# One core: the GpSimd drain in the last gate pair is taken out

## The chip, the core and the metric

The kernel runs on one core of one Trainium2 chip. The metric is device time in microseconds; lower is better. The times given are medians over several executions. The profile is one further execution, taken with the hardware profiler. The engines are named as in the profile: PE is TensorE (PEld its weight loads), DVE is VectorE, ACT is ScalarE, POOL is GpSimd, SP is SyncE, which only issues DMAs here.

## The reference

One layer of a streaming encoder trunk, over 2048 frames of a new stream (the prompt) and 32 further frames of a running one (the sample), with 1024 features, in float32:

```python
def layer(h, p, ...):
    proj = rmsnorm(h, g_mix) @ w_in
    hA, bA, cA, zA, vB, zB = jnp.split(proj, [...], axis=-1)
    yA, new_conv = short_conv_mixer(hA, bA, cA, zA, conv_hist, conv_w, conv_b)
    yB, new_pool = pooling_mixer(vB, zB, pool_hist, pos, pool_w, pool_scale)
    h = h + jnp.concatenate([yA, yB], axis=-1) @ w_out
    gate = jax.nn.sigmoid(rmsnorm(h, g_ple) @ w_ple_gate)
    h = h + (p @ w_ple) * gate
    return h, new_conv, new_pool
...
    return rmsnorm(h, g_final), ...
```

The part of interest is the end: the gate product with `w_ple_gate`, the sigmoid, the product of `p @ w_ple` (called the embedding, e) with the gate, the sum with h, and the final `rmsnorm` with `g_final`.

## The kernel before

Frames are cut into 16 tiles of 128 and a short one of 32. The kernel has three stages, one behind the other: the input projection with both mixers, the output projection with the residual, and the gate with the final norm. Every large product takes float32 operands that are split in two parts, high and low, and is made of three products of parts (`FINE`). Two tiles are always taken together as a pair, and the 2 x 2 blocks of a pair's matrix product are formed with seven block products in place of eight, by sums and differences of the blocks (function `seven`). Its three accumulators in PSUM are X, Y and Z. `carry` copies an accumulator out while it is still to be added to, `out` takes the finished block.

In the gate stage a loop runs over pairs 0, 2, ..., 12 with `gate_ops` and `done_g`; the last pair, tiles 14 and 15, has its own function `last_pair`. `done_g(i)` closes tile i: ScalarE squares h and sums it (`sumsq`, L94), GpSimd makes 1/sqrt of the mean in two small instructions (`rstd_of`, L73 and L77), VectorE scales the row (L1592), and a DMA stores it. For tile 13 `done_g` is called from within the last pair, as its step 3 (`before`).

`last_pair` works with these pieces, whose lines the profile names:

- L1670 (VectorE): adds an accumulator in PSUM to the carried copy; L1666 (ScalarE): the sigmoid of the result.
- L1633 and L1634 (VectorE): embedding times gate, and its sum with h (`gated`).
- L1638 (ScalarE) squares half a row of h and sums it, and GpSimd adds the sums (L1641, L1643) and takes the root (L1650).
- L1646: h times `g_bc`, on GpSimd for the first half of tile 14 (named hg, in `rest`), else on VectorE.
- L109 (TensorE): the embedding product of tile 15 (e_l), in `second`, with the weights wl that L123 loads again in four pieces; L1717: the seventh block product, in two halves of 256 columns (`end`).
- L1657 and L1659: the final scaling on VectorE and ScalarE, and L1658 and L1660 the stores, by SP and by ScalarE's queue.

The order of each engine's instructions is set when the program is built: a scheduler orders them by readiness, and `tc.keep_in_program_order` (here `fixed`) pins single ones to their place in the program. Each engine works through its own list in order, and waits for others through semaphores. `nc.gpsimd.drain()` at L1695 stands in the body of `last_pair`, ahead of the call of `seven`, and is pinned as well. It waits on no semaphore and posts none. In GpSimd's list it lies between the root of tile 12 (L77) and the first step of tile 13 (L73). GpSimd's own DMAs all come earlier in its list; the last is the store of tile 5. At the end of the program each engine has a closing sequence (put down to L1847), which on GpSimd begins with a drain and then has a handshake with the other engines, in which SP has waited for all stores.

Of the kernel before, what the change touches and what calls it, by code (L numbers as in the profile page):

```python
# [36 lines left out]
def trunk(ctx, tc, x_p, x_s, c_conv, c_pool, p_p, p_s, g_mix, w_in, conv_w, conv_b, pool_w,  # L37
          pool_scale, w_out, g_ple, w_gate, w_ple, g_fin, y_p, y_s, sc_p, sp_p, sc_s, sp_s):
    nc = tc.nc
# [1264 lines left out]
    with ExitStack() as s2:  # L1304
# [308 lines left out]
        def last_pair(i, A, before):  # L1613
# [15 lines left out]
            fixed = lambda ins: tc.keep_in_program_order(ins)  # L1629
# [62 lines left out]
            def rest():  # L1692
                of_first(cols_of(0), nc.gpsimd)

            fixed(nc.gpsimd.drain())  # L1695

            def second(cols):

                ps = bank(f"e_l{cols.start}")[:, :cols.stop - cols.start]
                embed_product(ps, pps, wp, cols)  # L1700
                return ps
# [109 lines left out]
        for i in range(0, NT - 3, 2):  # L1811
# [8 lines left out]
            if i + 2 < NT - 3:  # L1820
                done_g(i + 1, h[1])
        last_pair(NT - 3, S[NT - 3], lambda: done_g(NT - 4, h[1], True))

# [27 lines left out]
```

## Time and profile before

| | us |
|---|---|
| median of 3 runs | 913.25 (912.74 to 914.73) |
| profiled execution | 915.29 |
| span in the profile, first to last instruction | 913.5 |
| PE busy | 894.5 (98%) |
| DVE busy | 703.3 (77%) |
| ACT busy | 460.2 (50%) |
| POOL busy | 151.8 (17%) |
| DMA moved | 198.52 MB, of it 68.62 MB on GpSimd's queue (q0) |
| granted TensorE clock | 0.999 |

The profiled execution's own time is 1.8 us above its span, for what lies around the first and last instruction. In a row of the timeline stand the start in us from the span's start, the time in us, engine, line, operation, output<-inputs with their shapes, a count, and in brackets the idle time ahead of it with the instruction that ended it; "issue" stands there where the profile shows no releaser. A name with a q (POOLq, SPq) is an engine's instruction queue: what it only issues or waits with. Buffer numbers are left out of names, so c_g is the carried copy of several blocks.

### The profile page before, as it was taken

What the parts mean: (1) busy time and instruction counts of PE and PEld (TensorE: products, weight loads), DVE (VectorE), ACT (ScalarE), POOL (GpSimd) and SP (SyncE); (2) the same over time, 40 slices, a digit from 0 to 9 for tenths busy, and PEclk for the clock granted to TensorE, in tenths of its full rate; (3) what the DMA queues carried; (4) which work ended last, traced back from release to release, by engine and by line L of the source; (5) the groups of instructions that cost most, each with busy time, mean ns of one, the idle gap of its engine ahead of it and who ended that gap; (6) DMA issues with size and microseconds to landing.
All of it is one profiled execution on the core that took longest, in us unless ns stands there. A gap on an engine that the chain in (4) does not pass through costs nothing. (4 is left out here: it accounts for less than half of the span.)

```text
span 913.5 us, 12177 instructions
## 1 busy us (share of the span) xinstructions
PE 894.5 (98%) x4174; PEld 721.9 (79%) x4174; DVE 703.3 (77%) x1158; ACT 460.2 (50%) x834; POOL 151.8 (17%) x290
## 2 busy tenths in 40 slices
PE   8999999999999999999999999999999999999995
PEld 6788888888888778877788886888787778778884
DVE  6899799897993788746677679956557978897875
ACT  7744555554443354433343375643435865555553
POOL 2210122222131023100000021211112211110011
PEclk9999999999999999999999999999999999999999
DMA  8155286856699676767754595778678965565553
GB/s 277 52 187 173 81 265 201 243 170 210 194 346 428 154 221 188 231 208 253 241 150 147 184 357 164 269 218 283 214 241 285 315 226 184 178 227 191 187 207 144
DMA packets 113387, 198.52 MB, mean 217 GB/s; under 512 B 13174, under 2 KB 70062, under 8 KB 112429
## 3 DMA queue, kind: packets, MB, share of 16 engines
q1 hardware_dynamic: 91309, 124.72, 42.5%
q0 software_dynamic: 19568, 68.62, 22.3%
q10 hardware_dynamic: 2448, 4.39, 1.3%
q8 instruction: 33, 0.54, 0.2%
q14 instruction: 29, 0.24, 0.1%
HBM read 132.53 MB, written 65.15 MB: 216 GB/s over the span
## 5 line engine op out<-in xcount | busy, mean ns | idle before, releaser
L185 PE MATMUL z_o<-wo,y_S 128*128 128x512 f32 x192 | 47.4, 389 | 0.0
L185 PE MATMUL x_o<-wo_T,y_S 128*128 128x512 f32 x192 | 46.4, 391 | 0.7 <-DVE c_o L1319 0.7
L646 PE MATMUL x_zab<-B,w_zab_S 128*128 128x512 f32 x192 | 46.8, 392 | 0.2 <-DVE w_zab_S L84 0.2
L185 PE MATMUL z_g<-wg,g_S 128*128 128x512 f32 x192 | 46.8, 391 | 0.0
L646 PE MATMUL z_zab<-B,w_zab_S 128*128 128x512 f32 x192 | 46.8, 391 | 0.0
L185 PE MATMUL x_o<-wo,y 128*128 128x512 f32 x192 | 45.2, 389 | 0.0
L185 PEld LDWEIGHTS x_o<-wo_T,y_S 128*128 128x128 f32 x192 | 35.8, 188 | 9.0 <-DVE c_o L1319 1.6
L646 PEld LDWEIGHTS x_zab<-B,w_zab_S 128*128 128x128 f32 x192 | 35.8, 188 | 8.9 <-DVE w_zab_S L84 0.6
L185 PEld LDWEIGHTS x_o<-wo,y 128*128 128x128 f32 x192 | 36.0, 188 | 7.7
L646 PEld LDWEIGHTS z_zab<-B,w_zab_S 128*128 128x128 f32 x192 | 35.8, 188 | 7.8 <-DVE w_zab_S L84 0.3
L185 PEld LDWEIGHTS z_o<-wo,y_S 128*128 128x128 f32 x192 | 36.0, 188 | 7.5
L646 PE MATMUL x_ch<-B,w_ch_S 128*128 128x512 f32 x168 | 41.9, 392 | 0.0
L185 PEld LDWEIGHTS z_g<-wg,g_S 128*128 128x128 f32 x192 | 35.8, 188 | 7.5 <-ACT c_g L1573 0.2
L646 PE MATMUL x_zbv<-B,w_zbv_S 128*128 128x512 f32 x168 | 40.9, 392 | 0.6 <-ACT zs L986 0.6
L646 PE MATMUL z_zbv<-B,w_zbv_S 128*128 128x512 f32 x168 | 40.4, 390 | 0.0
L646 PE MATMUL z_ch<-B,w_ch_S 128*128 128x512 f32 x168 | 40.4, 389 | 0.0
L646 PEld LDWEIGHTS x_zbv<-B,w_zbv_S 128*128 128x128 f32 x168 | 31.3, 188 | 8.3 <-ACT zs L986 1.0
L646 PEld LDWEIGHTS x_ch<-B,w_ch_S 128*128 128x128 f32 x168 | 31.3, 188 | 7.3 <-ACT U L986 0.4
L646 PEld LDWEIGHTS z_ch<-B,w_ch_S 128*128 128x128 f32 x168 | 31.5, 188 | 6.6
L646 PEld LDWEIGHTS z_zbv<-B,w_zbv_S 128*128 128x128 f32 x168 | 31.5, 188 | 6.5
L81 ACT CAST y_S<-y_fS 128x512 fp32r<-128x512 f32 x28 | 16.9, 619 | 25.3 <-PE x_o L185 10.9
L1592 DVE SCALAR_TENSOR_TENSOR h<-h,rstd_f,g_bc 128x1024 f32<-128x1024 f32 (+1 forms) x15 | 19.2, 1280 | 12.2 <-POOL rstd_f L77 12.2
(552 smaller groups left out, 2281.0 us busy)
## 6 DMA issues: line engine op xcount, KB each, us to landing
wn<-in_w_in_dram SPq DMA_DIRECT2D x24, 512.0 KB, 5.3
y<-y_d SPq DMA_DIRECT2D x16, 512.0 KB, 6.9
p_dT<-T POOLq DMA_DIRECT2D x15, 512.0 KB, 5.1
e<-e_d SPq DMA_DIRECT2D x15, 512.0 KB, 4.3
x<-in_x_prompt_dram SPq DMA_DIRECT2D x14, 512.0 KB, 6.1
B<-p_d POOLq DMA_DIRECT2D x3, 2048.0 KB, 16.0
B<-p_dT POOLq DMA_DIRECT2D x3, 2048.0 KB, 21.9
h_d<-x SPq DMA_DIRECT2D x12, 512.0 KB, 7.5
```

The lines of the kernel that those rows point to most:

```text
L81: ins = nc.scalar.copy(hi, src)
L185: nc.tensor.matmul(ps[:n], lhs[:, k, a, :n], w[b][:, k], start=start and k + q == 0, stop=k == KH - 1 and q == 2, skip_group_check=True)
L646: nc.tensor.matmul(ps, lhs[:, k, x], b[:, k, y], start=start and k + q == 0, stop=stop and k == KH - 1 and q == 2, skip_group_check=True)
L1592: nc.vector.scalar_tensor_tensor(h[:n], h[:n], rf[:n], g_bc[:n], op0=ALU.mult, op1=ALU.mult)
```

## The change

One line of `last_pair` goes, the drain on GpSimd:

```diff
             def rest():
                 of_first(cols_of(0), nc.gpsimd)
 
-            fixed(nc.gpsimd.drain())
-
             def second(cols):
```

Nothing else is edited. GpSimd's list around the place, before (ms_f and rstd_f are the two steps of the root, of tile 12 in the first two rows and of tile 13 in the next two; the list leaves out instructions that only wait, and so the drain, which stood behind the second row):

```order
L73 TENSOR_SCALAR ms_f_7892<-ssq_f_7890 128x1
L77 TENSOR_TENSOR rstd_f_7894<-ms_f_7892,nhalf 128x1
L73 TENSOR_SCALAR ms_f_7966<-ssq_f_7964 128x1
L77 TENSOR_TENSOR rstd_f_7968<-ms_f_7966,nhalf 128x1
L1641 TENSOR_SCALAR ssq_l_0_7986<-ssq_l_0_7986 128x1
L1646 TENSOR_TENSOR hg_7906<-h_7902,g_bc 128x512
```

And now:

```order
L73 TENSOR_SCALAR ms_f_7892<-ssq_f_7890 128x1
L77 TENSOR_TENSOR rstd_f_7894<-ms_f_7892,nhalf 128x1
L73 TENSOR_SCALAR ms_f_7965<-ssq_f_7963 128x1
L77 TENSOR_TENSOR rstd_f_7967<-ms_f_7965,nhalf 128x1
L1641 TENSOR_SCALAR ssq_l_0_7985<-ssq_l_0_7985 128x1
L1646 TENSOR_TENSOR hg_7906<-h_7902,g_bc 128x512
```

The rows are the same; only the running numbers of buffers behind the drain are lower by one, and line numbers behind it by two. The lists of the other four engines, DMAs among them, keep every instruction at its place as well. GpSimd's program has 431 instructions before and 430 now, five drains before and four now: one at the start (L1838) and three in the closing sequence (L1847).

## The prediction

> **What bounds the kernel now.** I read the page's busy shares first, then the windows by stage, then TensorE's waits in the last 50 us, and then the timeline of the last pair engine by engine.
>
> ```profile
> PE 894.5 (98%) x4174; PEld 721.9 (79%) x4174; DVE 703.3 (77%) x1158; ACT 460.2 (50%) x834; POOL 151.8 (17%) x290
> 780.00:889.00 109.00, 109.00 (x499) 87.68 (x499) 92.01 (x135) 59.27 (x104) 14.66 (x27) 1.00 0.57 196
> 889.00:913.50 24.50, 15.12 (x82) 12.61 (x80) 14.11 (x21) 9.25 (x21) 5.15 (x12) 0.95 0.42 153
> PE x_g L1717 <- DVE c_g L1670: 2.4, 1, 2.4
> ```
>
> TensorE bounds the kernel until the last pair: in 780 to 889 us it is busy for all of 109.00 us. Of the last 24.5 us it fills only 15.12. There the order of work decides, and TensorE has one wait that counts: 2.4 us before L1717, for VectorE's L1670. So the question is what made that L1670 late. The timeline has the chain (start, duration, engine):
>
> ```profile
> 891.29 0.69 DVE L1670 TENSOR_TENSOR c_g<-y_g,c_g 128x512 f32<-128x512 f32 x1
> 891.39 0.20 ACT L94 ACTIVATION_READ_ACCUMULATOR junk<-h 128x1 f32 x1
> 889.50 0.55 POOL L77 TENSOR_TENSOR rstd_f<-ms_f,nhalf 128x1 f32<-128x1 f32 x1
> 894.59 0.19 POOL L73 TENSOR_SCALAR ms_f<-ssq_f 128x1 f32<-128x1 f32 x1 [4.54 <-issue]
> 894.86 0.55 POOL L77 TENSOR_TENSOR rstd_f<-ms_f,nhalf 128x1 f32<-128x1 f32 x1
> 895.44 1.28 DVE L1592 SCALAR_TENSOR_TENSOR h<-h,rstd_f,g_bc 128x1024 f32<-128x1024 f32 x1 [3.47 <-POOL rstd_f L77]
> 896.65 0.68 DVE L1633 TENSOR_TENSOR c_g<-e,c_g 128x512 f32<-128x512 f32 x1
> 897.37 0.69 DVE L1634 TENSOR_TENSOR h<-h,c_g 128x512 f32<-128x512 f32 x1
> 897.97 0.69 DVE L1670 TENSOR_TENSOR c_g<-z_g,c_g 128x512 f32<-128x512 f32 x1
> 898.86 0.71 ACT L1666 ACTIVATE c_g<-c_g,rs_h 128x512 f32<-128x512 f32 x1
> 899.60 1.56 DVE L1633 TENSOR_TENSOR c_g<-e,c_g 128x512 f32<-128x512 f32 x1 [0.94 <-ACT c_g L1666]
> 901.08 0.68 DVE L1670 TENSOR_TENSOR c_g<-x_g,c_g 128x512 f32<-128x512 f32 x1
> 901.82 1.69 PE L1717 MATMUL x_g<-wq,g 128*128 128x256 f32 x12 [2.37 <-DVE c_g L1670]
> ```
>
> Read it backwards. L1717 follows the L1670 of X (901.08), which stands in VectorE's order behind all rows above it, down to the L1592 of tile 13 at 895.44. That one sat idle 3.47 us for GpSimd's rstd, and GpSimd's first step for it (L73) began at 894.59. Its input, ScalarE's sum of squares, was done at 891.39 + 0.20 = 891.59. So L73 came 3.0 us after its data, and its bracket names no releaser ("issue"). What stands between the two on GpSimd is the instruction that the change removes:
>
> ```profile
> 889.46 0.60 POOLq L1695
> L1695 POOLq DRAIN  x1: 5012/5012/5012, 889.5 to 889.5; - x1
> L1847 POOLq DRAIN  x3: 34/98/677, 908.4 to 913.3; - x3
> L1838 POOLq DRAIN  x1: 168/168/168, 0.3 to 0.3; - x1
> ```
>
> The first row is from the chain of waits, the others from the views by source line. The drain of L1695 ran from 889.46 to 894.47. Only 0.6 us of that is the pow at 889.50, which ended at 890.05; 4.42 us are left over. The other four drains of GpSimd took 0.03 to 0.68 us, and the 0.68 covers a running pow of 0.57.
>
> **The change part by part.** One instruction goes. Nothing else moves on any queue, and the DMAs keep their places, so there are two terms: what the drain held up, and where its 4.42 us go.
>
> *Term 1, the front.* Without the drain L73 follows its data as its twin for tile 12 does: about 0.09 us after the sum, 891.68. From L73 to VectorE's L1592 the rows above take 895.44 - 894.59 = 0.85 us, so L1592 starts at 892.53, when VectorE has been free since 891.29 + 0.69 = 891.98. Step by step from there: L1633 at 892.53 + 1.21 = 893.74 (its sigmoid, the first row below, ended at 892.74) and L1634 from 894.46 to 895.15. Then VectorE is ahead of TensorE and waits for Z:
>
> ```profile
> 892.01 0.73 ACT L1666 ACTIVATE c_g<-c_g,rs_h 128x512 f32<-128x512 f32 x1 [0.42 <-DVE c_g L1670]
> 893.32 2.95 PE L185 MATMUL z_g<-wg,g_S 128*128 128x512 f32 x12
> 896.11 1.98 PE L185 MATMUL x_g<-wg_T,g_S 128*128 128x512 f32 x8
> 897.92 1.52 PE L109 MATMUL e_l<-wl,pps_l 128*128 128x512 f32 x6
> 899.35 1.26 POOL L1646 TENSOR_TENSOR hg<-h,g_bc 128x512 f32<-128x512 f32 x1
> ```
>
> Z is ready at 893.32 + 2.95 = 896.27, so L1670 of Z starts at 896.33, the sigmoid at 897.05, L1633 at 897.80 and the L1670 of X at 898.43 (X was ready at 896.11 + 1.98 = 898.09), done at 899.12. L1717 could go at 899.18. TensorE itself is then the later one: the six products of e_l began at 897.92 and go at 0.227 us each (the eight before them took 897.92 - 896.11 = 1.81), so they leave TensorE at 899.28. L1717 moves from 901.82 to 899.28: **-2.54 us**. From there to the end each wait hangs on TensorE's products, then on ScalarE, GpSimd and the last stores, and all of it shifts along. Bounds: the idle that the row prints, 2.37, and 2.64 if L1717 could follow L1670 at once.
>
> One price in it needs a look. GpSimd's L1646 (hg) took 1.26 us at 899.35, and the VectorE L1633 that met it, with two inputs in SBUF, took 1.56 us in place of 0.68: it ended 0.55 us after hg did, so it had waited. In the changed run hg moves along with L1634, behind which it began 1.98 us later, to 896.44, and ends at 897.70, just before L1633 at 897.80. It meets the L1670 of Z, whose one input is in PSUM. For that pair I have these rows, a pow at its normal length while VectorE reads PSUM:
>
> ```profile
> 593.26 0.69 DVE L1319 TENSOR_TENSOR c_o<-x_o,x 128x512 f32<-128x512 f32 x1 [1.37 <-PE x_o L185]
> 593.68 0.55 POOL L77 TENSOR_TENSOR rs_h<-ms_h,nhalf 128x1 f32<-128x1 f32 x1
> ```
>
> So I take no delay. If hg did hold the L1670 of Z to its end, that would start 1.37 later (897.70 for 896.33), the chain would give L1717 at 900.4 or so and term 1 would shrink to about -1.42. The Trainium skill, "GPSIMD Engine Reference", section "1. Specifications", has GpSimd share its SBUF interfaces with VectorE and clash with VectorE instructions that have two SBUF inputs; by that rule the L1670 of Z goes free, as in the rows, and the sum stays as it is.
>
> *Term 2, where the 4.42 us go.* GpSimd still has a drain at the end, at L1847. Whether it inherits them depends on what the long drain waited for. Its last DMA lay far back (first row; the other two are the first and the last of the list of its DMA issues, which come to 148):
>
> ```profile
> 812.32 0.57 POOL L1593 DMA_DIRECT2D out_dram<-h  x1 [1.09 <-DVE h L1592]
> p_dT<-T POOLq DMA_DIRECT2D x15, 512.0 KB, 5.1
> ...
> out_dram<-g_bc POOLq DMA_DIRECT2D x1, 4.0 KB, 8.6
> ```
>
> What sets the long drain apart from the other four is this: ahead of it GpSimd had issued all its 148 DMAs of the run, and no earlier drain lay between. The drain of L1838 stands before the first DMA; those of L1847 have none since L1695. 4.42 us over 148 is 30 ns each, the size of a short software step. So I take it that a GpSimd drain goes through the DMAs issued since the last drain, at 30 ns each, and that the first drain of L1847 now pays it. At the end of the kernel stands:
>
> ```profile
> 908.44 0.57 POOL L1650 TENSOR_TENSOR rstd_l<-ssq_l,nhalf 128x1 f32<-128x1 f32 x1
> L1847 SPq DRAIN  x3: 7/7/7, 912.7 to 913.0; - x3
> L1847 POOLq EVENT_SEMAPHORE  x4: 17/17/17, 912.8 to 913.4; - x4
> ```
>
> The last pow ends at 909.01. The stores behind it are waited for by SP, whose drain at 912.7 lets GpSimd's closing handshake begin at 912.8; 0.7 us later the span ends. Shifted by 2.54 the stores would allow the handshake at 910.26. The inherited drain ends at 909.01 - 2.54 + 4.42 = 910.89, the handshake is at 910.93: 3.75 of the 4.42 us lie under the last stores, and **+0.7 us** stick out. Bounds: 0 if the drain is short there (0.68 with the pow, as before), and +1.3 if the whole recorded 5.01 counts from the end of the pow.
>
> Sum: -2.54 + 0.7 = **-1.84 us**. The profiled execution, 915.29 us around its span of 913.5, becomes 913.45. The median of the runs, 913.25, lies 2.04 below the profiled one; the same difference makes it **911.4 us**, 0.2% less.
>
> The Trainium skill, "VectorE: DVE Perf Modes", section "The DRAIN you can't avoid", speaks against a gain: it gives the preamble's and postamble's drains as about 12 ns, constant, on all five engines. On GpSimd the rows differ (34 to 677 ns there, 5012 at L1695); for SP, at 7 ns, they agree. By the rule the time would not change.
>
> **The rivals.**
>
> *The cost does not reappear.* The 4.42 us belong to the place, where weight pieces and a store were in flight (rows below), and not to a backlog. For: nothing proves the 30 ns. Against: that traffic was SP's, not GpSimd's own. Then only term 1 counts: 913.25 - 2.54 = 910.7.
>
> *Half of the gain is lost on the way.* Either hg holds VectorE, as worked out, or the store of tile 13, which now issues near 893.9, delays the last weight piece:
>
> ```profile
> 892.17 0.32 SPq L123 DMA_DIRECT2D wl<-wl_d  x1
> 896.76 0.34 SPq L1593 DMA_DIRECT2D out_dram<-h  x1
> wl<-wl_d SPq DMA_DIRECT2D x4, 512.0 KB, 5.5
> out_dram<-h SPq DMA_DIRECT2D x2, 512.0 KB, 2.6
> ```
>
> At the median of 5.5 the piece lands at 897.7, and the fifth product of e_l needs it at 897.92 + 4 x 0.227 = 898.83, so 1.1 us of delay are free; a store that pushed it back by its whole 2.6 would cost 1.5. With -1.42 or -1.04 in front and the +0.7 behind, the time is 912.5 to 912.9.
>
> *Nothing changes.* The drain is long only under the profiler, or L73 was held by something else and stays there: 913.25.
>
> *Slower.* A drain waits for every store in flight, SP's and ScalarE's too, and only then spends its 4.42 us. For: at L1695 the store of tile 12, issued at 891.40, would land at 894.0 by the median of 2.6, near the drain's end at 894.47, and weight pieces were in flight before. Against: it would leave 0.5 us after that landing, not 4.42. Then in the changed run the last drain starts its work when the last store has landed (912.7 - 2.54 = 910.2), ends at 914.6, and with 0.7 behind it the span is 915.4: +1.9, 915.1. It decides from the point where the drain ends more than 2.54 us after the stores. Its milder form, no gain in front and a drain of 4.42 from 909.01 to 913.43, gives +0.7, 913.95.
>
> **How the numbers follow.** Forecast 0.50 (its own range 910.9 to 912.0), cost does not reappear 0.23, half lost 0.07, nothing 0.04, slower 0.16. About 0.2%, 1.83 us, is what a measurement of this kernel can tell from no change. The forecast lies on that line; I give it 0.30 beyond and 0.20 within, because of term 2's bounds the smaller price (a drain of 0.68 at this very place) has been measured and the larger has not. Faster: 0.30 + 0.23 = 0.53. Within: 0.20 + 0.07 + 0.04 + 0.02 of the slower case's mild form = 0.33. Slower: 0.14. The range goes from 910.4 (cost does not reappear, less a third of a microsecond of spread) to 913.6, and leaves out most of the slower case.
>
> **What would show it.** In the changed profile L73 of tile 13 should start near 891.7 with a bracket that names ScalarE's L94, L1592 near 892.5, and L1717 near 899.3 with no wait for L1670 worth speaking of. Term 2 is right if GpSimd's first L1847 drain takes about 5 us and the closing handshake waits for it, wrong if that row stays at 0.68. The forecast is wrong from the start if L73 stays near 894.6.

## The result, and the profile after

| | before | changed |
|---|---|---|
| median, us | 913.25 (911.37 to 914.73, 6 runs) | 909.67 (909.16 to 911.01, 6 runs) |
| ratio of the times | | 0.9964, 95% interval 0.9951 to 0.9976 |
| profiled execution, us | 915.29 | 909.97 |
| its span, us | 913.5 | 908.2 |

The change is faster by 0.4%. The direction and the mechanism came as forecast; the time lies 1.7 us below the 911.4 and 0.7 us below the low end of the range.

First the last pair of the changed kernel, as a timeline (start, duration, engine, line, operation, and in brackets the idle time ahead with its releaser). Lines behind the change are lower by two, so L1717 of before is L1715 here:

```profile
886.10 0.55 POOL L77 TENSOR_TENSOR rstd_f<-ms_f,nhalf 128x1 f32<-128x1 f32 x1
886.27 2.88 PE L185 MATMUL z_g<-wg,g_S 128*128 128x512 f32 x12
887.97 0.19 ACT L94 ACTIVATION_READ_ACCUMULATOR junk<-h 128x1 f32 x1
888.24 0.19 POOL L73 TENSOR_SCALAR ms_f<-ssq_f 128x1 f32<-128x1 f32 x1 [1.59 <-ACT junk L94]
889.10 1.28 DVE L1592 SCALAR_TENSOR_TENSOR h<-h,rstd_f,g_bc 128x1024 f32<-128x1024 f32 x1 [0.53 <-POOL rstd_f L77]
...
892.90 0.69 DVE L1670 TENSOR_TENSOR c_g<-z_g,c_g 128x512 f32<-128x512 f32 x1 [1.19 <-PE z_g L185]
893.01 1.30 POOL L1646 TENSOR_TENSOR hg<-h,g_bc 128x512 f32<-128x512 f32 x1
894.39 0.69 DVE L1633 TENSOR_TENSOR c_g<-e,c_g 128x512 f32<-128x512 f32 x1 [0.79 <-ACT c_g L1666]
894.52 1.52 PE L109 MATMUL e_l<-wl,pps_l 128*128 128x512 f32 x6
894.99 0.69 DVE L1670 TENSOR_TENSOR c_g<-x_g,c_g 128x512 f32<-128x512 f32 x1
895.88 1.60 PE L1715 MATMUL x_g<-wq,g 128*128 128x256 f32 x12
902.41 0.57 POOL L1650 TENSOR_TENSOR rstd_l<-ssq_l,nhalf 128x1 f32<-128x1 f32 x1
```

The bracket of L73 now names ScalarE's sum of squares, where it said "issue" before: the instruction waits for its data and for nothing else. The bracket ahead of TensorE's seventh block product, 2.37 us before, is gone.

The two executions cannot be compared by clock times, since the changed one reached the last pair earlier. So I count from the first Z product of the last pair, at 889.70 before and 886.27 after. That product lies ahead of everything the drain holds up. The windows from there to the end of the span (busy time of PE, PEld, DVE, ACT, POOL, then the granted clock, DMA share and GB/s), first of before, then of the changed kernel:

```profile
889.70:913.50 23.80, 14.42 (x79) 12.04 (x77) 13.74 (x20) 9.25 (x21) 4.53 (x11) 0.95 0.40 149
```

```profile
886.27:908.20 21.93, 14.20 (x79) 12.10 (x77) 12.95 (x20) 9.36 (x21) 4.60 (x11) 0.91 0.44 161
```

The same work takes 23.8 us before and 21.9 after: **1.9 us less in the last pair**. The other 3.4 us of the difference between the two profiled executions lie ahead of it, where both kernels run the same program.

The closing sequence of the changed kernel, from its view by source line (count, then shortest, median and longest in ns, first and last start):

```profile
L1845 POOLq EVENT_SEMAPHORE  x4: 17/17/17, 907.5 to 908.1; - x4
L1845 POOLq DRAIN  x3: 46/98/5026, 902.4 to 907.9; - x3
L1845 SPq DRAIN  x3: 7/7/7, 906.7 to 907.7; - x3
```

The 5 us have moved here. SP was through with the stores at 906.7, but GpSimd's drain ran from 902.4 to 907.4, and the handshake began at 907.5. Before, SP was done at 912.7 and the handshake came at 912.8. So 0.7 us of the drain stick out.

### The profile page after: what moved, and what is told of

The parts are those of the page before. It is cut to its first block, busy times and chain, and to the rows that moved or that the text cites. A ratio compares the mean times of both kernels' runs of the same rounds, so it can differ in the third digit from the quotient of the medians.

```text
span 908.2 us, 12176 instructions
## 1 busy us (share of the span) xinstructions
PE 893.2 (98%) x4174; PEld 722.8 (80%) x4174; DVE 702.4 (77%) x1158; ACT 460.1 (51%) x834; POOL 152.0 (17%) x290
## 4 chain that ended last, share of the span: by engine, by line
PE 73%; issue 11%; DMA 8%; DVE 3%; ACT 2%; POOL 2%; POOLq 0%; DVEq 0%; ACTq 0%
PE x_g L185 9%; PE x_o L185 8%; PE x_zab L646 6%; PE x_zbv L646 6%; PE x_ch L646 6%; PE z_g L185 5%; PE z_o L185 4%; DMA raw_zab_0b<-in_w_in_dram 4%; PE z_zab L646 3%; PE z_ch L646 3%; PE z_zbv L646 3%; PE e L109 2%; PE y_g L185 2%; PE y_o L185 2%; DMA B<-p_d 2%
## 5 line engine op out<-in xcount | busy, mean ns | idle before, releaser
L81 ACT CAST y_S<-y_fS 128x512 fp32r<-128x512 f32 x28 | 17.0, 620 | 28.1 <-PE x_o L185 12.2
L1319 DVE TENSOR_TENSOR c_o<-x_o,x 128x512 f32<-128x512 f32 x14 | 9.6, 689 | 21.8 <-PE x_o L185 21.8
```

Of the source, the lines that this page charges most:

```text
L81: ins = nc.scalar.copy(hi, src)
L1319: add = lambda o, a, b: nc.vector.tensor_tensor(o, a, b, op=ALU.add)
```

## The experiments

In what follows "length" is the time from the first Z product of the last pair to the end of the span, and "L73" the start of tile 13's L73 counted from that product. "Left after the pow" is a drain's recorded time less 0.59 us: the drain is recorded from 0.04 us ahead of a pow of 0.55 us, and ended behind it in every run.

**The same program again, and the change again.** Two kernels, timed 12 times each beside 35 runs of before: before without any edit, and the change as it stands.

> The kernel before, unchanged, timed against itself: how far do two sets of runs of one program differ? Theory 1 (the drain accounts for 1.9 us of the 3.6, the rest is scatter between executions in the work ahead of the last pair): sets may differ by 1 to 2 us, a ratio up to 0.2% from 1. Theory 2 (taking the instruction out also makes the work ahead of the last pair faster by about 1.7 us, every time): sets of one program agree within 0.1%, 0.999 to 1.001.

> The changed kernel once more. Theory 1: the ratio comes nearer to 0.998 (-1.9 us) than 0.9964; the profile again shows -2.5 us up to the last product and a drain of about 5.0 us in the closing sequence. Theory 2: 0.996 again (-3.5 us), and in the profile a last pair that is 1.9 us shorter with the rest gained ahead of it.

Before, run again: median 913.65 us (912.0 to 917.93), ratio 1.0005 (0.9991 to 1.002). Its timeline, where the columns are as above:

```profile
886.72 2.88 PE L185 MATMUL z_g<-wg,g_S 128*128 128x512 f32 x12
891.63 0.19 POOL L73 TENSOR_SCALAR ms_f<-ssq_f 128x1 f32<-128x1 f32 x1 [4.54 <-issue]
898.86 1.70 PE L1717 MATMUL x_g<-wq,g 128*128 128x256 f32 x12 [2.38 <-DVE c_g L1670]
```

The first Z product stands at 886.72 with the drain still in the program, 3.0 us earlier than in the first profile of before and only 0.45 later than in the changed kernel. So those 3 us ahead of the last pair are scatter between executions: before reaches the earlier time too. Over half of it arises where the output projection gives way to the gate stage: between 700 and 740 us TensorE is busy for 38.4 us in the first profile of before, and for all 40 in this one and in the first of the change. Inside the last pair the two profiles of before agree: L73 at +4.91 (4.89 in the first profile), and with a span of 910.6 us the length is 23.9 (23.8). The two timed sets of before agree within 0.1%, which was theory 2's forecast for them; the change, run again, shows sets of one kernel further apart.

The change, run again: median 911.28 us (908.68 to 913.94), ratio 0.9971 (0.9959 to 0.9984). Its timeline:

```profile
886.32 2.88 PE L185 MATMUL z_g<-wg,g_S 128*128 128x512 f32 x12
895.93 1.60 PE L1715 MATMUL x_g<-wq,g 128*128 128x256 f32 x12
```

With a span of 908.2 us the length is 21.9, and the product follows at +9.61, as in the first profile of the change; the first drain of the closing sequence takes 5.03 us again. The six runs of the result had a mean of 909.80, these twelve 911.26: sets of one kernel differ by 1.5 us. The ratio of 0.9971 lies midway between the 0.998 of theory 1 and the 0.9964 of theory 2, so the timed sets decide for neither. The profiles speak for theory 1: the change is worth 1.9 us in the last pair, and before, run again, comes as early to that pair with the drain as the changed kernel without it.

**The place kept, the waiting taken out.** A one-element memset on GpSimd stands where the drain stood, pinned in the same way.

```diff
-            fixed(nc.gpsimd.drain())
+            fixed(nc.gpsimd.memset(warm, 0.0))
```

> In place of the drain a memset of one column on GpSimd (0.1 us): GpSimd's list is as long as before, but nothing is drained there. Theory 1: the time of the changed kernel within 0.1%; GpSimd's root for tile 13 follows its data by 0.1 to 0.3 us; closing drain 5.0 us. Theory 2 in the form that the length of GpSimd's list matters: 1.7 us slower than the changed kernel, about 911.4.

Median 910.73 us (908.79 to 914.46), ratio 0.9971 (0.9958 to 0.9983). The timeline:

```profile
886.98 2.88 PE L185 MATMUL z_g<-wg,g_S 128*128 128x512 f32 x12
887.27 0.10 POOL L1695 MEMSET warm<- 128x1 f32 x1
888.95 0.19 POOL L73 TENSOR_SCALAR ms_f<-ssq_f 128x1 f32<-128x1 f32 x1 [1.58 <-ACT junk L94]
```

An instruction at this place costs 0.10 us and holds nothing up; L73 comes at +1.97, as in the change, the closing drain takes 5.03 us, and with a span of 908.9 us the length is 21.9 again. It is the drain that held GpSimd, not the place or the pinning.

**The drain moved to where GpSimd is idle.** The old drain goes, and a new one stands behind the last DMA that GpSimd issues, after tiles 4 and 5, some 77 us ahead of the last pair.

```diff
-            fixed(nc.gpsimd.drain())
...
+            if i == 4:
+                tc.keep_in_program_order(nc.gpsimd.drain())
```

> The drain stands right behind GpSimd's last DMA (the store of tile 5, issued near 810 us), where GpSimd has nothing to do for about 12 us. Theory 1 (a GpSimd drain goes through the DMAs issued since the last drain, 148 here, about 30 ns each, and only once): the drain there takes 5 to 8 us unseen, the closing drain 0.7 us, the gain in front stays, and the time is 0.7 us below the changed kernel's. Rival (the cost belongs to the place, or the closing drain costs 5 us anyway): closing drain 5 us and the time of the changed kernel.

Median 910.61 us (909.42 to 913.13), ratio 0.997 (0.9958 to 0.9981). The first row is the moved drain, the second the closing sequence:

```profile
L1822 POOLq DRAIN  x1: 10131/10131/10131, 809.1 to 809.1; - x1
```

```profile
L1848 POOLq DRAIN  x3: 34/98/675, 902.5 to 907.3; - x3
```

The closing drain is back at 0.68 us, so one earlier drain takes the whole price off the end. Behind it GpSimd had nothing to do until 821, so the 10.13 us cost nothing. They are longer than the 5 us of the old place, and than the 5 to 8 that were expected. A store of GpSimd's was issued at 809.10, right ahead, and landed 7.9 us later, at 817.0; the drain ended at 819.2, 2.2 us behind it. Two kernels further down (0 DMAs between, and 16 tiny stores) have a drain at the same place:

```profile
L1823 POOLq DRAIN  x1: 7041/7041/7041, 810.1 to 810.1; - x1
```

```profile
L1823 POOLq DRAIN  x1: 6665/6665/6665, 809.5 to 809.5; - x1
```

There the same store was issued at 810.16 and 809.52 and took 4.8 and 4.4 us to land, and the drain ended 2.2 us after that in both. So a drain of GpSimd also waits for GpSimd's own stores that are still under way. From the first Z product at 886.38 the length of the kernel with the moved drain is 21.2, another 0.7 us less than in the change. That is the size of the piece that sticks out there. The timed runs don't separate the two kernels (910.61 and 911.28, intervals that overlap).

**What the drain counts.** My term 2 had 30 ns for each of 148 DMAs. The next kernels keep the drain at its old place and put a second one further ahead, so that a known number of GpSimd's DMAs lies between the two. The second drain stands behind the store of tile 5 (0 DMAs between), behind the store of tile 0 (8), ahead of the gate stage (22), and at the start of the output projection (50). Each kernel has one of these; the last line serves for the third and the fourth, at its two places:

```diff
+            if i == 4:
+                tc.keep_in_program_order(nc.gpsimd.drain())
...
+            if i == 0:
+                tc.keep_in_program_order(nc.gpsimd.drain())
...
+        tc.keep_in_program_order(nc.gpsimd.drain())
```

> Two drains: one right behind GpSimd's last DMA and the one of before at its place. Between them lie no DMAs. Theory 1 (30 ns for each DMA since the last drain, once): the drain at the old place ends within 0.1 us of the pow ahead of it, so it is about 0.6 us long; closing drain 0.7; from the start of the last pair's Z product to the end of the span 21.2 us, as with the early drain alone. Rival (the cost belongs to the place): 5.0 us again at the old place and 23.8 us.

> An extra drain behind the store of tile 0, with 8 DMAs of GpSimd between it and the drain at the old place. Theory 1: the drain at the old place ends 0.24 us + about 0.05 after the pow ahead of it; last pair 21.2 us. Rival (place): 4.4 us after it, 23.8 us.

> An extra drain at the start of the gate stage, with 22 DMAs of GpSimd between it and the drain at the old place. Theory 1: the drain at the old place ends 0.66 us + about 0.05 after the pow; last pair 21.2 us. Rival (place): 4.4 us after it, 23.8 us.

> An extra drain at the start of the output projection, with 50 DMAs of GpSimd between it and the drain at the old place. Theory 1: the drain at the old place ends 1.5 us + about 0.05 after the pow; that is at the time when the input of tile 13's root is ready, so the last pair is still 21.2 to 21.3 us. Rival (place): 4.4 us after it, 23.8 us.

The drain at the old place, in the views by source line of the four kernels in this order:

```profile
L1695 POOLq DRAIN  x1: 660/660/660, 887.5 to 887.5; - x1
```

```profile
L1695 POOLq DRAIN  x1: 1322/1322/1322, 885.7 to 885.7; - x1
```

```profile
L1697 POOLq DRAIN  x1: 2466/2466/2466, 887.6 to 887.6; - x1
```

```profile
L1696 POOLq DRAIN  x1: 4754/4754/4754, 888.2 to 888.2; - x1
```

Left after the pow are 0.07, 0.73, 1.88 and 4.17 us: 0.07 and then **82 ns for each DMA**, in a straight line, and not 30. The time hangs on GpSimd's DMAs since the last drain, so the backlog was right and its price was not. At 82 ns each, the 4.42 us of before are the price of 53 DMAs, not of 148. The lengths are 21.2, 21.2, 21.3 and 24.9 us, and the closing drain took 0.67 to 0.68 us in all four. The first three came within 0.1 us of the forecast. The 24.9, forecast at 21.2 to 21.3, did not: at 82 ns the drain held L73 until +4.64, and a part of the excess is of another kind (see the longer gap, below). One execution of each took 910.77, 908.96, 910.89 and 915.29 us, beside 913.85 of before.

**Count or bytes, and how many stay on the books.** Three kernels. In the first, sixteen stores of 4 bytes each are added behind the early drain, with the old drain kept. In the second, the same sixteen are added to before without an early drain (164 DMAs in all). In the third, a second drain is put into the input projection, so that 64 DMAs follow it and 84 precede it. The edits of the first and the third (the second has the first without its drain):

```diff
+            if i == 4:
+                tc.keep_in_program_order(nc.gpsimd.drain())
+                scr = tc.dram_tile([16, 8], F32, name="scr")
+                for k in range(16):
+                    tc.keep_in_program_order(nc.gpsimd.dma_start(scr[k:k + 1, :1], nhalf[:1, :1]))
...
+                if gi == 1 and j == 3:
+                    tc.keep_in_program_order(nc.gpsimd.drain())
```

> Drain early and at the old place, as in the run with both, and between them 16 extra DMAs of GpSimd of 4 bytes each (they write to a scratch tensor that nothing reads). The runs so far gave 0.07 us after the pow for 0 DMAs, 0.73 for 8, 1.88 for 22, 4.17 for 50: 0.082 us each. By the count of DMAs: 0.07 + 16 x 0.082 = 1.38 us. By their bytes or pieces (one piece each, where the 8 had 128 rows of 4 KB): under 0.2 us.

> The kernel before with the same 16 DMAs of 4 bytes ahead of the drain, and no early drain. With all 148 DMAs the drain took 4.42 us after the pow, which is 53 at 0.082. If a limit on the number of DMAs that are still on the books sets that, 4.42 again. If the limit is one of room that small DMAs hardly take up, up to 4.42 + 16 x 0.082 = 5.7 us. If every DMA counts and the first ones are only cheaper, 4.9 us (164 at 0.030).

> An extra drain late in the input projection, with 64 DMAs between it and the drain at the old place. Straight line: 0.07 + 64 x 0.082 = 5.3 us after the pow. Limit at about 53 DMAs: 4.42 us, as with 148.

The drain at the old place in the three, and in the last fence the added drain of the third:

```profile
L1695 POOLq DRAIN  x1: 1976/1976/1976, 889.6 to 889.6; - x1
```

```profile
L1695 POOLq DRAIN  x1: 6317/6317/6317, 886.7 to 886.7; - x1
```

```profile
L1697 POOLq DRAIN  x1: 5899/5899/5899, 885.6 to 885.6; - x1
```

```profile
L1294 POOLq DRAIN  x1: 4368/4368/4368, 380.8 to 380.8; - x1
```

| kernel | DMAs since the last drain | left after the pow, us | 0.07 + 0.082 x DMAs |
|---|---|---|---|
| drain behind tile 5 | 0 | 0.07 | 0.07 |
| drain behind tile 0 | 8 | 0.73 | 0.73 |
| 16 tiny stores | 16 | 1.39 | 1.38 |
| drain ahead of the gate | 22 | 1.88 | 1.87 |
| drain at the output projection | 50 | 4.17 | 4.17 |
| drain in the input projection | 64 | 5.31 | 5.32 |
| before | 148 | 4.42 | 12.2 |
| before and 16 tiny stores | 164 | 5.73 | 13.5 |

Sixteen stores of 4 bytes cost what sixteen large ones would, so it is the count and not the bytes. Added to before, they add 5.73 - 4.42 = 1.31 us, 82 ns each again, so 53 is no upper limit on the count. But of the 148 only so much is paid as 53 would cost, while with a drain behind the 84th all 64 that follow do. That added drain itself took 4.37 us, which at 82 ns has room for 53 DMAs at the most, with 84 issued ahead of it. So some DMAs are off the books already there, in the input projection, without a drain. What takes them off, these runs don't tell.

One execution of each took 912.93, 915.05 and 913.64 us, beside 913.08 of before.

**A longer gap on TensorE.** In three of the kernels above (50 and 64 DMAs between, and 164) the last pair was longer than the move of the seventh block product explains. From 888.46 to 913.4 the kernel with 50 took 24.9 us, 1.1 more than before, though its drain was shorter. With 64 the product came 0.9 later than before (+12.99) and the end 2.3, with 164 it came 1.3 later (+13.42) and the end 2.6. The windows show why: its rows for one step of the clock with the gap of TensorE, and for the next step:

```profile
898.13:901.54 3.41, 1.31 (x11) 1.21 (x11) 3.38 (x5) 1.23 (x3) 1.00 (x1) 1.00 0.02 5
901.54:904.96 3.42, 3.42 (x19) 3.42 (x18) 3.05 (x7) 1.75 (x6) 0.97 (x3) 0.50 0.23 85
```

The granted clock (third number from the end) changes here in steps of 3.41 us. In the first step TensorE was busy for 1.31 us, and the next one ran at 0.50. Two such windows of before run again, whose gap of 2.38 us is longer but lies across a step's boundary, which leaves 1.72 us of work in the step that holds most of it:

```profile
897.16:900.58 3.42, 1.72 (x14) 1.72 (x15) 3.39 (x5) 1.38 (x3) 0.69 (x2) 1.00 0.02 5
900.58:903.99 3.41, 2.96 (x24) 2.71 (x23) 3.01 (x7) 2.57 (x7) 0.92 (x3) 1.00 0.39 144
```

There the clock stays at 1.00. To test it, the next kernel makes the gap longer: the drain of before, and twenty memsets pinned behind it.

```diff
             fixed(nc.gpsimd.drain())
+            for _ in range(20):
+                fixed(nc.gpsimd.memset(warm, 0.0))
```

> The kernel before with 20 memsets of one column on GpSimd behind the drain (0.1 us each), which hold the root of tile 13 for 2 us more. In the run with 50 DMAs TensorE's idle gap of 2.1 us fell into one of the 3.4 us steps in which the granted clock changes, and the next step ran at half the clock, 1.1 to 1.4 us lost. Theory (an idle gap of TensorE halves the clock of the next step): with a gap of about 4.4 us such a step always comes, and the last pair takes 23.8 + 2.0 + 1.1 to 1.4 = 26.9 to 27.2 us. Rival (the half step was chance in that one run): full clock to the end of the products and 25.8 us.

The timeline, then two steps of the clock:

```profile
895.27 3.06 POOL L1697 MEMSET warm<- 128x1 f32 x20 [4.50 <-issue]
905.65 2.93 PE L1719 MATMUL x_g<-wq,g 128*128 128x256 f32 x12 [5.47 <-DVE c_g L1670]
909.23 1.61 PE L1719 MATMUL x_g<-wq,g 128*128 128x256 f32 x12
```

```profile
901.85:905.26 3.41, 0.00 (x0) 0.00 (x0) 2.47 (x4) 1.33 (x3) 1.50 (x2) 1.00 0.25 101
905.26:908.67 3.41, 3.02 (x14) 3.02 (x15) 3.34 (x6) 1.43 (x4) 0.76 (x2) 0.50 0.02 5
```

The twelve products behind the gap took 2.93 us, their twins at full clock 1.61. The product starts at +15.23 from the first Z product (890.42), 3.1 later than before, but the length (span 918.6) is 28.2, 4.4 more: 1.3 us are the half step. (The forecast length was 26.9 to 27.2, because the memsets were taken for 2 us; they took 3.06.) The time was 920.53 us. So a gap of TensorE there costs itself, and then another 1.2 to 1.4 us when a clock step holds too much of it. The 14 profiles agree on where the limit lies. Once the clock has first reached 1.00, which is within 12 us of the start, every step of 3.41 us with 1.42 us of TensorE's work or less is followed by a step at 0.50, and every step with 1.72 us or more by one at 1.00; none lies between.

## Why the prediction was right in its steps and off in its time

**What holds L73, and term 1: right.** L73 was to follow at 891.68, which is +1.98 from the first Z product; it came at +1.97. L1592 was to come at +2.83 and did. The seventh block product was to start at +9.58, behind TensorE's own six products of e_l; it started at +9.61. Before it was +12.12: -2.51 for the -2.54 of the term. The memset at the old place shows that only the drain did it.

**hg and VectorE: right.** hg was to move to +6.74 and did (893.01), and ran beside the L1670 of Z, with 0.69 us for it as always: no delay. And the L1633 that met hg before and took 1.56 us then takes 0.69. The rule of the Trainium skill that was weighed there ("GPSIMD Engine Reference", section "1. Specifications") agrees with these rows.

**Term 2: the sum right, its unit price wrong.** The closing drain took over the whole 5.03 us, and the end came 0.6 us later behind the seventh product (11.7 us to the end before, 12.3 after), for +0.7. The 30 ns were my division of 4.42 by 148; the measured price is 82 ns for a DMA that still counts, and the 4.42 us are the price of 53. What GpSimd does in the 82 ns, no run shows. The sum didn't need the split, since the same DMAs are on the books at the end. The rule of "VectorE: DVE Perf Modes", section "The DRAIN you can't avoid" (the Trainium skill), by which the postamble's drains are some 12 ns on every engine, does not hold for GpSimd behind DMAs of its own: 5026 ns here.

**The rivals.** The cost did reappear, which rules out the first; moving the drain to an idle place shows what it was worth (0.7 us). Nothing of term 1 was lost on the way, L73 did move, and the closing drain ran beside the stores of SP and ScalarE and not behind them: it began at 902.4 and SP was through with the stores at 906.7. The timed sets moved as well as the profile, which speaks against a drain that is long under the profiler alone. One sum of a rival was off: with hg in the way, the prediction's own steps give L1717 at 899.18 + 1.37 = 900.55 and term 1 at -1.27, not -1.42; hg held up nothing, so nothing hangs on it.

**The sum: right for the place, -1.84 against -1.9 measured.**

**What failed** is the last step, "the same difference makes it 911.4 us", with a range whose low end allowed "a third of a microsecond of spread". It took the last pair's difference for the whole difference of two medians, and two things were missing: the spread was put at a third of a microsecond where sets of runs differ by 1.5, and a half step of the clock behind the gap was put at nothing.

The first is scatter, and it is shown. Executions of one program differ by 1 to 2 us or more in work that is the same: the first Z product of before stood at 889.70 in one execution and at 886.72 in the next. Over all 14 profiles it stands at 885.81 to 890.42 with a drain at the old place (ten of them) and at 886.27 to 886.98 without (four); so few don't exclude that its mean moves a little with the change. The six runs of the result came out low, with a mean 1.5 below the next twelve of the same kernel. In the longer set, on one chip, 47 runs of before have a mean of 913.72, and 24 of the change and its twin with the memset 911.16: a difference of 2.6, with a standard error of 0.4, where the first sets gave 3.3.

The second is a term that the sum left out: the gap of 2.37 us that the drain put in front of the seventh product sometimes costs a half-clock step on top, which the change removes with the gap. That gaps do this is shown by four kernels; how often it happened in the unprofiled runs of before is an estimate. TensorE idle for 1.70 us of a step (1.72 busy) left the clock alone, 1.99 us (1.42 busy) did not. If the steps fall on the gap at random, the share of executions in which one step holds at least L us of a gap of 2.37 is (3.41 + 2.37 - 2 x L)/3.41: 53% for a limit L of 1.99, 70% for 1.70. At 1.3 us each that is 0.7 to 0.9 us on the mean. Sorting the 47 runs by mean granted clock gives less: 17 at 0.997 or below have a mean of 914.5, the other 30 of 913.3, which is 17/47 x 1.2 = 0.45 us. The 1.2 between the two groups (standard error 0.4) is the size of one half step, and the 30 alone lie 2.1 above the 911.16, near the 1.9 of the profiles. But the mean clock doesn't say where in a run it was low, so this is an estimate too. With 0.45 to 0.9 the change is worth 2.3 to 2.8 us, and the 2.6 measured on one chip lies in it. The two profiled executions of before did not happen to have such a step, so their profiles could not show it.

The Trainium skill states on this point ("TensorE: Matmul & The Clock Gate", section "Part 1: The HAM clock gate (the "warmup" mystery)") that the clock is halved after an idle window of about 3.4 us and that this window runs freely. The steps of 3.41 us agree with its length. But no whole idle window was needed here: 1.31 and 1.42 us of work in the step did not keep the clock up.

Open are what takes DMAs off GpSimd's books in the input projection, what makes the work ahead of the last pair scatter and whether its mean moves with the change, and how often a half step of the clock fell behind the gap in the timed runs of before.

## What to carry to other kernels

A drain on GpSimd pays for the DMAs that GpSimd itself has issued since its last drain (82 ns each here, for up to 64 of them), and if it is taken out, the next drain pays, at the latest the one that closes the kernel. Put it where GpSimd has nothing to do and its transfers have landed, and never between a reduction and the engine that waits for its root: with the drain there the last pair took 23.8 us here, with none 21.9, and with one at an idle place 21.2. Where the total scatters by more than the change is worth, measure the stage from a fixed instruction to the end: it repeated to 0.1 us between the profiles of one kernel, where the means of two sets of its runs lay 1.5 apart. And count a gap of TensorE with the clock step that it may halve.

## What was not expected of the hardware

- The price of a GpSimd drain goes by the number of GpSimd's DMAs: 0.07 us and 82 ns each, for 4-byte stores and for large ones alike (0, 8, 16, 22, 50 and 64 DMAs fit within 0.01 us). Of 148 without a drain between, only the price of 53 was paid.
- A drain that comes while GpSimd's own stores are under way waits for them: right behind the store of tile 5 it took 10.13, 7.04 and 6.67 us in three kernels, and ended 2.2 us after that store's landing in each.
- The granted clock went to 0.50 for the next step of 3.41 us after a step in which TensorE was busy for 1.42 us or less, and stayed at 1.00 after 1.72 or more. The products in the half step took 2.93 us where they take 1.61.
